# Expert weights in sheets of two pages with rows of 16 KB, GpSimd's work of the attention moved to VectorE, and a last norm summed in PSUM

## The chip, the cores and the metric
The kernel runs on one core of a Trainium2 chip. The core has five engines: TensorE (PE, matmuls; PEld is its weight load), VectorE (DVE), ScalarE (ACT), GpSimd (POOL) and SyncE (SP, which here issues nearly all DMA transfers). Sixteen DMA engines move data between HBM and SBUF. The metric is the device time of one execution in microseconds (us), the median of the runs. "us" positions are counted from the start of the profiled span.

## The reference
One encoder layer on 512 tokens of 1024 channels, all in float32. A conditioning vector gives shift, scale and gate rows for both halves (`sh, sc, g`). The first half is attention with two groups of heads (8 latent heads, 4 differential heads with a relative-position bias), an output projection and a layer norm. The second half is what the change touches most:

```
u   = x * (1 + sc_f) + sh_f
aff = softmax(u @ w_router)                      # 16 experts
g, idx = top_k(aff.T, 64)                        # each expert picks 64 of 512 tokens
xs  = u[idx]                                     # (16, 64, 1024)
h   = silu(xs @ w_gate) * (xs @ w_up)            # w_gate, w_up: (16, 1024, 2048)
y   = (h @ w_down) * g                           # w_down: (16, 2048, 1024)
ffn = zeros.at[idx].add(y)                       # back to the 512 tokens
out = layer_norm(ALPHA * x + g_f * ffn, ln2_g, ln2_b)
```

Each expert has three matrices of 8 MB, 403 MB in all, and each is read once.

## The kernel before, in words
SBUF is cut into 24 pages of 128 partitions x 8 KB (class `Pages`). Every larger tile takes a page or a half or quarter of one by `pages.get()` and gives it back by `pages.put()`; a page is the oldest free one.

**Up to the routing (0 to 340 us).** Stage 1 projects the input; then a loop over 32 steps `s` runs the scores, softmax and values of the 16 differential blocks (`s` 0 to 15) and the 16 latent blocks (`s` 16 to 31), with projections filled in between. Float32 operands of matmuls are split in a high and a low part (`split`: ACT rounds, another engine subtracts, L237). GpSimd subtracts for the queries (`q_proj`), the normalised latents (`lat_norm`), the value weights (`wk_load`) and the output weights (`wo_split`, which also multiplies by the gate row at L734). `W0, WD = 9, 3` say at which steps the first four blocks of the output weights are split (9, 12, 15, 18). This part has no order written by hand: the compiler's planner orders each engine's instructions by simulated times. From the second norm's sums on, sections marked `manual_schedule` keep the written order on each engine. The routing ends in a search of the 65th largest affinity (`DVE.max` and `match_replace`, L1192 to L1194) and the one-hot matrices that gather the chosen tokens.

**The experts (340 to 1278 us).** The 16 experts go in 8 pairs (`pr`); two experts of a pair use the two halves of TensorE's columns at once. For each pair, `up` runs eight blocks `k` of 128 channels for w_gate, then eight for w_up, and `down` eight blocks `b` of 256 FF rows for w_down. One block of one expert is 1 MB: one page, one DMA of 128 rows of 8 KB. Between blocks stand the scatter of the pair before (in the gate part), the gather of the next pair (in the down part) and the transposes of the hidden values (`hidden_t`). `prefetch` walks one list (`stream`, 392 loads) and issues the next load on SP whenever a page is free; `turn` gives back the pages of a used block and calls it. The list begins to move at `s` = 29 with `keep=3` pages left over, and after the routing with none. During pair 0 eight pages leave the stock for other tiles (tokens, gate rows, hidden values, their transposes, norm rows, two of accumulators; `take_xs` to `take_acc`); one comes back in pair 1. In the last pair w_down is read in two column halves for its second half (16 loads of 512 KB in rows of 2 KB).

**The last norm (`finish`).** After the last down matmul DVE gates the result, PE scatters it, and DVE, ACT and GpSimd share the sums, the inverse root and the scaling of the 512 x 1024 output; SP stores it in eight pieces.

Of the kernel before, what the change touches and what calls it, by code (L numbers as in the profile page):

```python
# [21 lines left out]
W0, WD = 9, 3  # L22
# [4 lines left out]
NPAGES = 24  # L27
NWARM = 384
# [25 lines left out]
class Pages:  # L54
    def __init__(self, pool, n):
        self.pool = pool
        self.t = [None] * n
        self.kind = [None] * n
        self.used = [0] * n
        self.stamp = [[0] * 4 for _ in range(n)]  # L60
        self.now = 0
        self.peak = 0

    def get(self, kb=8, kind=F32, old=False):
        need = kb // 2
        best = None
        for i, u in enumerate(self.used):
            if u and self.kind[i] != kind:
                continue
            for off in range(0, 4 - need + 1, need):  # L70
# [4 lines left out]
                key = (age, u == 0) if old else (u == 0, age)  # L75
# [5 lines left out]
        if not self.used[i]:  # L81
            self.now += 1
            self.kind[i] = kind
            self.t[i] = self.pool.tile([P, 2048], kind, name=f"pg{i}_{self.now}", tag=f"pg{i}", bufs=1)
# [3 lines left out]

    def put(self, h):
        i, m = h  # L90
        assert self.used[i] & m == m
        self.used[i] &= ~m
        self.now += 1
        for k in range(4):
            if m >> k & 1:
                self.stamp[i][k] = self.now

    def free(self):
        return sum(u == 0 for u in self.used)
# [3 lines left out]
def encoder_layer(ctx: ExitStack, tc: tile.TileContext, xT, x, wadaT, cvec, colp, rowp, rows, cst, pos, posr,  # L103
# [5 lines left out]
    pagep = ctx.enter_context(tc.tile_pool(name="pagep", bufs=1))  # L109
# [4 lines left out]
    pages = Pages(pagep, NPAGES)  # L114
# [492 lines left out]
    def lat_evac(j, bank):  # L607
# [5 lines left out]
        if j == 1:  # L613
            POOL.tensor_tensor(s, s, lat[0][3], op=OP.add)
# [28 lines left out]
    def wk_load():  # L643
# [3 lines left out]
        WK["vh"], WK["v"] = split(raw[:, 512:], 512, POOL)  # L647
# [54 lines left out]
    def q_proj(h, bank):  # L702
# [8 lines left out]
        QM[h] = split(f, 512, DVE if h < 0 else POOL)  # L711
# [28 lines left out]
    def x_load():  # L740
        for t2 in range(2):
            h, pg = pages.get()
# [20 lines left out]
    Gc, Bc = fixed.tile([P, 8], F32, name="Gc"), fixed.tile([P, 8], F32, name="Bc")  # L763
    wrg = rowb[:, :256].rearrange("p (k e) -> p k e", k=KB)
# [147 lines left out]

# [14 lines left out]

    NP = NEXP // 2
    stream = []
    for pr in range(NP):  # L930
        for w, nm in ((w_gate, "g"), (w_up, "u")):
            for k in range(KB):
                for e in range(2):
                    off = w.offset + ((2 * pr + e) * D + k * P) * FF
                    stream.append(((pr, nm, k, e), bass.AP(tensor=w.tensor, offset=off, ap=[[FF, P], [1, FF]])))
        for b in range(KB if pr < NP - 1 else KB // 2):
            for e in range(2):
                off = w_down.offset + ((2 * pr + e) * FF + b * 2 * P) * D
                stream.append(((pr, "d", b, e), bass.AP(tensor=w_down.tensor, offset=off, ap=[[2 * D, P], [1, 2 * D]])))

    for c in range(2):
        for b in range(KB // 2, KB):
            for e in range(2):
                off = w_down.offset + ((2 * (NP - 1) + e) * FF + b * 2 * P) * D + c * 512
                stream.append(((NP - 1, c, b, e), bass.AP(tensor=w_down.tensor, offset=off, ap=[[2 * D, P], [D, 2], [1, 512]])))
    stream.reverse()
    loaded = {}

    def prefetch(keep=0):
        while stream and pages.free() > keep:  # L950
            key, src = stream.pop()
            n = math.prod(src.shape[1:])
            h, pg = pages.get(n // 256)
            SP.dma_start(pg.rearrange("p (j n) -> p j n", j=2) if len(src.shape) == 3 else pg, src)
            loaded[key] = (h, pg)
# [101 lines left out]
    for s in range(NU):  # L1057
# [42 lines left out]
        if s in MODS or s >= 18:  # L1100
            mod_step()
        if s in EARLY:
            prefetch(EARLY[s])
# [26 lines left out]
    prefetch(KEEP)  # L1130
# [53 lines left out]
    prefetch()  # L1184
# [5 lines left out]

    for r in range(8):
# [36 lines left out]
    def gather(pr, banks, k0=0, k1=KB):  # L1228
        oh = OHh[0].rearrange("p (t s) -> p t s", t=4)
        xs = XS[pr % 2]  # L1230
        for k in range(k0, k1):
            src = banks[k % 2][:, (k // 2) * P:(k // 2 + 1) * P]
            for t in range(4):
                mm(src, Z[t][:, k * P:(k + 1) * P], oh[:, t, :], t == 0, t == 3)
            if k % 2:
                ACT.activation(xs[:, k, :], src, AF.Identity, scale=Gc[:, k:k + 1], bias=Bc[:, k:k + 1])
            else:
                DVE.tensor_scalar(xs[:, k, :], src, Gc[:, k:k + 1], Bc[:, k:k + 1], op0=OP.mult, op1=OP.add)  # L1238
# [36 lines left out]
    def take_rows():  # L1275
        EP["gbh"], gb = pages.get()
        EP["gb"] = gb
# [22 lines left out]
    def last_rows():  # L1300
        _, l2 = pages.get()
        SP.dma_start(l2[0:1, :], bass.AP(tensor=rows.tensor, offset=rows.offset + 2048, ap=[[2048, 1], [1, 2048]]))
        EP["l2"] = l2
# [12 lines left out]
    def up(pr, nm, banks, between, columns=None):  # L1316
# [269 lines left out]
```

## Time and profile before

| what | value |
|---|---|
| time, median of 3 runs | 1303.66 us (1299.6 to 1304.99) |
| time of the profiled execution | 1303.92 us |
| its span, first to last instruction | 1302.1 us |
| mean granted TensorE clock | 0.969 |
| busy: PE, DVE, ACT, POOL | 1185.2, 373.8, 225.0, 118.7 us |
| moved by DMA | 456.1 MB, mean 350 GB/s |

A row of the profile names an engine, a line of the kernel (L12 is line 12), what is written and read, and the number of instructions. "Busy" counts time in instructions; for PE it is not the same as work at full rate. The granted clock is 1.00 at 2.4 GHz and 0.50 at 1.2 GHz.

### The profile page before, as it was taken

Reading aid. Unit: us, or ns where it says so; the run is one execution under the profiler, and the core shown is the slowest. Engines: PE = TensorE matmul, PEld = TensorE weight load, DVE = VectorE, ACT = ScalarE, POOL = GpSimd, SP = SyncE. Lnnn points to the kernel's source line nnn. Section 1 sums busy time; section 2 is a strip of 40 time slices with the busy share of each in tenths; the row PEclk is TensorE's granted clock in tenths of the full one; section 3 lists DMA queues with packets and bytes.
Section 4 is the critical chain, followed back from the end, with each engine's and each line's share of the span. In section 5 each row is a group of like instructions: output and inputs, shape, how many; then the busy total and the mean of one; then the engine's idle time right before and its main releaser. Section 6 shows DMA issues by size and latency. Waiting matters only on the chain.

```text
span 1302.1 us, 13908 instructions
## 1 busy us (share of the span) xinstructions
PE 1185.2 (91%) x5581; PEld 550.5 (42%) x5581; DVE 373.8 (29%) x793; ACT 225.0 (17%) x464; POOL 118.7 (9%) x79
## 2 busy tenths in 40 slices
PE   8899888999899999998899799879978997998793
PEld 5677556777433433432342243224323432432231
DVE  6798897636301111020110012010101110110107
ACT  3465665542210000000000000000000000000000
POOL 2500532320000500000000000000000000000002
PEclk9899998999999999999999999999998999999987
DMA  9775531374999899999999999999999999999981
GB/s 345 291 231 194 176 138 65 130 283 154 385 385 420 335 422 421 421 421 421 421 422 421 421 422 421 421 421 421 422 421 421 420 421 422 421 422 421 422 304 65
DMA packets 76215, 456.10 MB, mean 350 GB/s; under 512 B 8140, under 2 KB 8524, under 8 KB 28018
## 3 DMA queue, kind: packets, MB, share of 16 engines
q1 hardware_dynamic: 75858, 455.08, 86.3%
q8 instruction: 44, 0.72, 0.2%
q14 instruction: 23, 0.19, 0.0%
q10 hardware_dynamic: 290, 0.10, 0.0%
HBM read 453.04 MB, written 3.95 MB: 351 GB/s over the span
## 4 chain that ended last, share of the span: by engine, by line
DMA 45%; PE 27%; DVE 2%; issue 0%; ACT 0%; SPq 0%; DVEq 0%
DMA pg<-in_w_up_dram 19%; DMA pg<-in_w_gate_dram 15%; PE bk L122 14%; PE bk L1322 11%; DMA pg<-in_w_down_dram 11%; PE bk L1353 1%; DVE pg L1427 0%; DVE pg L1418 0%; DVE small L1192 0%; DVE ohg L1194 0%; DVE lst L1412 0%; DVE lst L162 0%; PE bk L1243 0%; DVE mv L165 0%; PE bk L1271 0%
## 5 line engine op out<-in xcount | busy, mean ns | idle before, releaser
L122 PE MATMUL bk<-pg,pg 128*128 128x512 f32 (+4 forms) x2282 | 530.9, 490 | 13.6 <-POOL pg L423 4.4
L122 PEld LDWEIGHTS bk<-pg,pg 128*64 128x64 f32 (+2 forms) x2282 | 259.7, 163 | 237.5 <-issue 176.3
L1322 PE MATMUL bk<-pg,pg 128*64 128x512 f32 x1024 | 242.8, 609 | 35.1 <-DMA pg<-in_w_up_dram 33.6
L1322 PE MATMUL bk<-pg,xs 128*64 128x512 f32 x1024 | 241.0, 605 | 30.3 <-DMA pg<-in_w_up_dram 30.0
L1322 PEld LDWEIGHTS bk<-pg,pg 128*64 128x64 f32 x1024 | 73.6, 139 | 193.3 <-issue 128.5
L1322 PEld LDWEIGHTS bk<-pg,xs 128*64 128x64 f32 x1024 | 73.3, 138 | 183.0 <-issue 124.3
L1347 DVE TENSOR_TENSOR pg<-pg,bk 128x512 f32<-128x512 f32 x32 | 22.0, 688 | 405.0 <-PE bk L1322 405.0
L144 ACT ACTIVATE pg<-bk 128x512 f32<-128x512 f32 (+1 forms) x105 | 59.3, 583 | 434.2 <-PE bk L1353 353.7
L1226 POOL TENSOR_TENSOR ohg<-ohg,aff 128x512 f32<-128x512 f32 x8 | 8.4, 1049 | 789.5 <-DVE ohg L1225 789.5
L1249 DVE TENSOR_TENSOR pg<-pg,bk 128x512 f32<-128x512 f32 x60 | 41.3, 688 | 124.7 <-PE bk L122 124.4
L122 PEld LDWEIGHTS bk<-ohg,pg 128*128 128x128 f32 x512 | 61.3, 196 | 28.8 <-issue 28.8
L122 PE MATMUL bk<-ohg,pg 128*128 128x128 f32 x512 | 67.9, 286 | 0.5 <-DVE ohg L1225 0.5
L1343 ACT ACTIVATE pg<-bk 128x512 f32<-128x512 f32 x32 | 18.8, 598 | 241.3 <-PE bk L1322 241.3
L137 ACT ACTIVATE pg<-pg 128x512 fp32r<-128x512 f32 (+2 forms) x63 | 42.8, 708 | 26.0 <-DVE pg L710 7.0
L237 POOL TENSOR_TENSOR pg<-pg,pg 128x512 fp32r<-128x512 f32 (+1 forms) x20 | 34.8, 1745 | 91.6 <-ACT pg L137 91.5
L1008 DVE CUSTOM_DVE_ANT_0 pg<-pg,pg 128x1024 f32<-128x1024 f32 x32 | 39.7, 1276 | 2.3 <-DMA pg<-in_wadaT_dram 2.2
L1238 DVE TENSOR_SCALAR xs<-bk,Gc,Bc 128x128 f32<-128x128 f32 x16 | 6.6, 410 | 100.1 <-PE bk L122 100.1
L1238 DVE TENSOR_SCALAR pg<-bk,Gc,Bc 128x128 f32<-128x128 f32 x16 | 6.6, 410 | 97.7 <-PE bk L122 97.7
L122 PE MATMUL bk<-pg 64*128 64x512 f32 (+3 forms) x94 | 30.5, 485 | 3.2 <-DMA pg<-in_cvec_dram 2.2
L1386 DVE TENSOR_TENSOR pg<-bk,pg 128x512 f32<-128x512 f32 x16 | 11.1, 692 | 67.5 <-PE bk L122 67.5
L1353 PEld LDWEIGHTS bk<-csb,pg 128*128 128x128 f32 x128 | 17.8, 209 | 26.1 <-issue 22.8
L218 DVE CUSTOM_DVE_ANT_0 pg<-pg,pg 128x1024 f32<-128x1024 f32 x16 | 25.7, 1640 | 5.7 <-DMA pg<-in_wadaT_dram 5.7
(211 smaller groups left out, 629.4 us busy)
## 6 DMA issues: line engine op xcount, KB each, us to landing
pg<-in_w_gate_dram SPq DMA_DIRECT2D x128, 1024.0 KB, 19.8
pg<-in_w_up_dram SPq DMA_DIRECT2D x128, 1024.0 KB, 19.8
pg<-in_w_down_dram SPq DMA_DIRECT2D x120, 1024.0 KB, 19.8
pg<-in_wadaT_dram SPq DMA_DIRECT2D x16, 1024.0 KB, 7.3
pg<-in_wadaT_dram SPq DMA_DIRECT2D x16, 512.0 KB, 6.2
pg<-in_w_down_dram SPq DMA_DIRECT2D x16, 512.0 KB, 10.8
pg<-bias_d SPq DMA_DIRECT2D x16, 256.0 KB, 4.8
pg<-in_w_out_dram SPq DMA_DIRECT2D x8, 512.0 KB, 3.2
```

What stands on the lines that cost most here:

```text
L122: PE.matmul(o, l, r, start=start, stop=stop)
L137: return ACT.activation(dst, src, AF.Copy, scale=scale)
L144: ACT.activation(dst, src, AF.Copy)
L218: DVE.tensor_tensor_reduce(out=w2[:, j], in0=w2[:, j], in1=cs, scale=1.0, scalar=0.0, op0=OP.mult, op1=OP.add, accum_out=modr[:, n:n + 1])
L237: lo_eng.tensor_tensor(lo, src, ff(hi), op=OP.subtract)
L1008: DVE.tensor_tensor_reduce(out=w2[:, j], in0=w2[:, j], in1=cs, scale=1.0, scalar=0.0, op0=OP.mult, op1=OP.add, accum_out=modr[:, n:n + 1])
L1238: DVE.tensor_scalar(xs[:, k, :], src, Gc[:, k:k + 1], Bc[:, k:k + 1], op0=OP.mult, op1=OP.add)
L1249: DVE.tensor_add(acc[t][:, c], acc[t][:, c], bank)
L1322: PE.matmul(banks[c][r], xs[:, k, r], w[e][:, c * 512:(c + 1) * 512], start=k == 0, stop=k == 7)
L1343: ACT.activation(EP["HS"][:, c * 512:(c + 1) * 512], banks[c], AF.Silu)
L1347: DVE.tensor_tensor(s, s, U[c], op=OP.mult)
L1353: PE.transpose(G[c % 2][:, i * P:(i + 1) * P], sj[:, i // 2, i % 2, :], ident)
```

## The change
**Sheets.** From the top of the 24 pages, two neighbouring free pages are turned into a "sheet" of 128 partitions x 16 KB the first time one is wanted. One load of the stream is now 2 MB: partition p holds two neighbouring channels of w_gate or w_up (256 channels in a block), or four neighbouring FF rows of w_down (512 in a block), 16 KB in one run. The tokens are gathered with every second column (`k // 2 * 256 + k % 2 :: 2`) and the hidden values transposed with every fourth, so that the contraction fits; the gate scale and shift columns are regrouped for it (`GBp`). A sheet is used in two halves and given back after the second. The lowest ten pages (`LOW`) serve other tiles; pages 0 and 1 are kept for x, and from step 18 (`LATE`) tiles are put into the low pages first. In the first fill a 2 MB load may also go to two low pages as two DMAs of 8 KB rows; later loads go to sheets. The page of the first norm's rows is kept and reloaded with the last norm's rows (`l2`).

**GpSimd.** All its subtractions, products and the sum between stage 1 and the routing go to DVE; `W0, WD = 15, 1` splits the first output weights at steps 15 to 18.

**The end.** The last norm's rows are spread to all partitions in gate step 6 of the last pair (before: behind down block 1). In `finish` each token block's first half is multiplied by the norm's scale row early, and its bias and mean terms are summed by matmuls with diagonal matrices in PSUM; DVE does the second halves; GpSimd is not used.

The diff, cut:

```diff
-W0, WD = 9, 3
+W0, WD = 15, 1
+LOW = 10
+LATE = 18
 class Pages:
-    def get(self, kb=8, kind=F32, old=False):
+    def get(self, kb=8, kind=F32, old=False, first=2, top=None):
...
-                key = (age, u == 0) if old else (u == 0, age)
+                high = self.late and (0 if i < self.low else i - self.low + 1)
+                key = (age, u == 0) if old else (high, u == 0, age) if self.late else (u == 0, age)
...
+    def has_sheet(self):
+        n = len(self.used)
+        return any(not u for u, _, _ in self.sheets) or n > self.low and not self.used[n - 1] and not self.used[n - 2]
+    def sheet(self):
+        free = [x for x in self.sheets if not x[0]]
+        if free:
+            x = min(free, key=lambda x: x[1])
+        else:
+            for v in (self.used, self.stamp, self.t, self.kind):
+                del v[-2:]
+            self.pools.pop().release()
+            i = len(self.sheets)
+            x = [0, 0, self.open(f"sheet{i}", bass.Side.RIGHT if hasattr(bass.Side, "RIGHT") else "right")]
+            self.sheets.append(x)
...
-            POOL.tensor_tensor(s, s, lat[0][3], op=OP.add)
+            DVE.tensor_tensor(s, s, lat[0][3], op=OP.add)
-        LN_[j] = split(c, 512, POOL)
+        LN_[j] = split(c, 512, DVE)
-        WK["vh"], WK["v"] = split(raw[:, 512:], 512, POOL)
+        WK["vh"], WK["v"] = split(raw[:, 512:], 512, DVE)
-        QM[h] = split(f, 512, DVE if h < 0 else POOL)
+        QM[h] = split(f, 512, DVE)
-        POOL.tensor_tensor(raw, raw, GR["r"], op=OP.mult)
-        WOh[k], WO[k] = split(raw, 1024, POOL)
+        DVE.tensor_tensor(raw, raw, GR["r"], op=OP.mult)
+        WOh[k], WO[k] = split(raw, 1024, DVE)
...
+    def block(w, ex, rows, b, n):
+        return bass.AP(tensor=w.tensor, offset=w.offset + (ex * rows + b * n * P) * (4096 // n), ap=[[4096, P], [1, 4096]])
...
+    def prefetch(keep=0, low=0):
+        while stream and (not keep or pages.free() - 2 * (not begun) >= keep):
+            key, src = stream[-1]
+            if not begun and pages.has_sheet() and not (low == 2 and pages.free(LOW)):
+                h, pg = pages.sheet()
...
+            elif (begun or low) and pages.free(LOW):
+                h, pg = pages.get(top=LOW)
+                SP.dma_start(pg, bass.AP(tensor=src.tensor, offset=src.offset + 2048 * len(begun), ap=[[4096, P], [1, 2048]]))
...
-            prefetch(EARLY[s])
+            prefetch(EARLY[s], 1)
-    prefetch(KEEP)
+    prefetch(KEEP, 1)
-    prefetch()
+    prefetch(0, 2)
+    for h in range(2):
+        for j in range(2):
+            for i, v in enumerate((Gc, Bc)):
+                mm(BK[4][64 * h:64 * h + 64, 8 * i + j:8 * i + j + 7:2], ident[:, j:127 + j:2], v[:, h:h + 7:2], True, True)
...
-            (0, "u", 5): take_rows, (0, "d", 2): lambda: take_acc(0), (0, "d", 4): lambda: take_acc(1),
-            (1, "g", 0): lambda: pages.put(EP["gbh"]), (NP - 1, "g", 7): last_rows}
+            (0, "u", 5): take_rows, (0, "d", 1): lambda: take_acc(0), (0, "d", 3): lambda: take_acc(1),
+            (NP - 2, "d", KB - 1): last_rows}
...
+        n = KB if columns is None else KB - 1
+        for k in range(KB):
+            if k % 2 == 0:
+                h, w = zip(*(loaded.pop((pr, nm, k // 2, e)) for e in range(2)))
...
+            turn(pr, nm, k, h[0][k % 2] + h[1][k % 2])
...
+    def finish_first(t):
         scatter(NP - 1, t, 0, TB[t % 2])
+        a = acc[t][:, :512]
+        DVE.bn_stats(lst[:, 24 * t:24 * t + 6], a)
+        DVE.tensor_tensor(a, a, EP["l2"][:, :512], op=OP.mult)
     def finish():
...
+        bias(0)
+        gated(1, YB)
+        bias(1)
+        for t in range(4):
+            mm(LB[t], OHT[(NP - 1) % 2][:, t * P:(t + 1) * P], EP["YS"][:, 512:], False, True)
+            DVE.bn_stats(lst[:, 24 * t + 6:24 * t + 12], LB[t])
+            DVE.bn_aggr(mv2[:, 2 * t:2 * t + 2], lst[:, 24 * t:24 * t + 12].rearrange("p (c s) -> p c s", s=6))
...
+        for t in range(4):
+            ACT.activation(diag[:, t], ident, AF.Copy, scale=nb[:, t:t + 1])
+            mm(banks[t], diag[:, t], l2[:, :512], False, t == 3)
+            if t < 3:
+                ACT.activation(diag[:, 4 + t], ident, AF.Copy, scale=rs[:, t:t + 1])
+                mm(banks[t], diag[:, 4 + t], acc[t][:, :512], False, True)
+        for t in range(4):
+            centre(t)
+            scaled(t)
...
+            elif k == 6 and pr == NP - 1:
+                spread(EP["l2"], U[2:], (1.0, 1.0))
...
-                if b == 1:
-                    spread(EP["l2"], TB, (1.0, 1.0))
```

## Rows read from the trace of the kernel before
**Rows 1.** Windows: PE, PEld, DVE, ACT, POOL busy (count), granted clock, DMA share, GB/s.
```profile
500.00:1100.00 600.00, 546.89 (x2468) 202.44 (x2464) 65.46 (x105) 30.06 (x55) 5.25 (x5) 0.99 1.01 421
```
**Rows 2.** Chain that ended last: start us, length us, what.
```profile
488.90 15.62 DMA pg<-in_w_up_dram
...
1207.35 17.35 DMA pg<-in_w_up_dram
```
**Rows 3.** Window in the down part of pair 0.
```profile
430.00:440.00 10.00, 10.00 (x62) 5.53 (x60) 0.82 (x2) 0.92 (x2) 4.42 (x3) 1.00 0.76 288
```
**Rows 4.** Window of the loads with rows of 2 KB.
```profile
1247.00:1259.00 12.00, 12.00 (x38) 3.56 (x38) 0.69 (x1) 0.00 (x0) 0.00 (x0) 0.82 1.05 387
```
**Rows 5.** Timeline of SP's issues: start us, length us, count.
```profile
271.77 51.40 SPq L954 DMA_DIRECT2D pg<-in_w_gate_dram  x13
...
456.61 32.68 SPq L954 DMA_DIRECT2D pg<-in_w_up_dram  x16
```
**Rows 6.** Timeline of PE, pairs 0 and 1; a step is 16 matmuls.
```profile
366.05 7.09 PE L1322 MATMUL bk<-pg,xs 128*64 128x512 f32 x32
...
444.91 7.09 PE L122 MATMUL bk<-pg,pg 128*64 128x512 f32 x32
...
458.01 3.65 PE L1322 MATMUL bk<-pg,pg 128*64 128x512 f32 x16
```
**Rows 7.** Timeline of PE, last pair; in brackets idle before and its releaser.
```profile
1199.87 8.78 PE L1322 MATMUL bk<-pg,pg 128*64 128x512 f32 x32 [2.40 <-DMA pg<-in_w_up_dram]
...
1242.44 5.29 PE L122 MATMUL bk<-pg,csb 1*128 1x512 f32 x8
1247.66 5.50 PE L122 MATMUL bk<-pg,pg 128*64 128x512 f32 x16
1253.09 1.98 PE L122 MATMUL bk<-pg,csb 128*128 128x512 f32 x4
```
**Rows 8.** Timeline of DVE, last norm.
```profile
1278.12 0.69 DVE L1386 TENSOR_TENSOR pg<-bk,pg 128x512 f32<-128x512 f32 x1 [0.46 <-PE bk L122]
...
1287.39 1.23 DVE L165 TENSOR_SCALAR mv<-mv 128x2 int32<-128x2 int32 x1
...
1298.34 0.68 DVE L1435 TENSOR_TENSOR pg<-pg,pg 128x512 f32<-128x512 f32 x1
```
**Rows 9.** Windows of the tail.
```profile
1240.00:1250.00 10.00, 10.00 (x26) 2.91 (x24) 1.38 (x2) 1.19 (x2) 0.00 (x0) 0.73 1.04 390
...
1290.00:1302.00 12.00, 0.00 (x0) 0.00 (x0) 8.92 (x15) 0.78 (x1) 4.29 (x3) 0.50 0.41 154
```
**Rows 10.** Groups by line: names, shapes, count | busy us, mean ns | idle before.
```profile
L237 POOL TENSOR_TENSOR pg<-pg,pg 128x512 fp32r<-128x512 f32 (+1 forms) x20 | 34.8, 1745 | 91.6 <-ACT pg L137 91.5
...
L734 POOL TENSOR_TENSOR pg<-pg,pg 128x1024 f32<-128x1024 f32 x8 | 21.0, 2635 | 11.6 <-DMA pg<-in_w_out_dram 10.3 <-ACT pg L144 1.3
...
L237 DVE TENSOR_TENSOR pg<-pg,pg 128x1024 fp32r<-128x1024 f32 x7 | 9.4, 1361 | 1.5 <-ACT pg L137 1.5
```
**Rows 11.** Timelines of DVE and PE, 120 to 210 us.
```profile
122.61 1.35 DVE L162 TENSOR_TENSOR st<-st 128x4 f32<-128x4 f32 x2
...
146.72 2.30 DVE L168 SCALAR_TENSOR_TENSOR small<-small 128x8 f32<-128x8 f32 x1
...
149.07 1.11 PE L631 MATMUL bk<-csb,small 128*128 128x128 f32 x4 [3.99 <-DVE small L168]
...
208.79 2.20 DVE L571 SCALAR_TENSOR_TENSOR pg<-pg,st,rowb 128x128 f32<-128x128 f32 x4
```
**Rows 12.** Windows, 120 to 320 us.
```profile
120.00:180.00 60.00, 52.10 (x298) 37.77 (x298) 52.83 (x130) 38.94 (x95) 29.11 (x15) 0.97 0.40 136
180.00:220.00 40.00, 32.11 (x175) 23.15 (x175) 33.80 (x79) 20.57 (x48) 2.65 (x2) 0.87 0.35 126
220.00:320.00 100.00, 100.00 (x692) 78.21 (x688) 52.72 (x121) 46.52 (x107) 25.20 (x12) 1.00 0.47 177
```
**Rows 13.** Timeline of PE: four transposes with step two.
```profile
1228.83 0.75 PE L1353 MATMUL bk<-csb,pg 128*128 128x128 f32 x4
```

More of the change, by code (lines that the diff above doesn't have):

```diff
@@ L54, with __init__ @@
 class Pages:
-    def __init__(self, pool, n):
-        self.pool = pool
+    def __init__(self, tc, ctx, n, low):
+        self.tc, self.ctx, self.low = tc, ctx, low
+        self.pools = [self.open(f"pages{i}", bass.Side.LEFT if hasattr(bass.Side, "LEFT") else "left") for i in range(n // 2)]
+        self.sheets = []
         self.t = [None] * n
@@ L62, in __init__, with open @@
         self.peak = 0
-    def get(self, kb=8, kind=F32, old=False):
+        self.late = False
+    def open(self, name, side):
+        pool = self.tc.tile_pool(name=name, bufs=1, side=side).__enter__()
+        self.ctx.callback(lambda: pool._released or pool.release())
+        return pool
+    def get(self, kb=8, kind=F32, old=False, first=2, top=None):
         need = kb // 2
         best = None
-        for i, u in enumerate(self.used):
-            if u and self.kind[i] != kind:
+        for i, u in enumerate(self.used[:top]):
+            if i < first or u and self.kind[i] != kind:
                 continue
@@ L87, in get @@
         return (i, m), self.t[i][:, off * 512:(off + need) * 512]
+    def has_sheet(self):
[12 more added lines that the diff above has]
+            self.sheets.append(x)
+        i = next(j for j, y in enumerate(self.sheets) if y is x)
+        self.now += 1
+        x[0] = 1
+        return ("sheet", i), x[2].tile([P, 4096], F32, name=f"sh{i}_{self.now}", tag=f"sh{i}", bufs=1)
     def put(self, h):
         i, m = h
+        self.now += 1
+        if i == "sheet":
+            assert self.sheets[m][0]
+            self.sheets[m][:2] = [0, self.now]
+            return
         assert self.used[i] & m == m
         self.used[i] &= ~m
-        self.now += 1
         for k in range(4):
@@ L96, in put, with free @@
                 self.stamp[i][k] = self.now
-    def free(self):
-        return sum(u == 0 for u in self.used)
+    def free(self, top=None):
+        return sum(u == 0 for u in self.used[:top])
 @with_exitstack
@@ L741, in x_load @@
         for t2 in range(2):
-            h, pg = pages.get()
+            h, pg = pages.get(first=0, top=2)
             Zh.append(h)
@@ L941, in encoder_layer @@
     for c in range(2):
[L942 to L945, printed above, removed]
+        for b in range(2, 4):
+            stream.append(((NP - 1, c, b), [bass.AP(tensor=w_down.tensor, offset=w_down.offset + ((2 * (NP - 1) + e) * FF + b * 512) * D + c * 512,
+                                                    ap=[[4 * D, P], [D, 4], [1, 512]]) for e in range(2)]))
@@ L946, in encoder_layer @@
     stream.reverse()
     loaded = {}
[L949 to L955, printed above, removed]
+    begun = []
+    def prefetch(keep=0, low=0):
[3 more added lines that the diff above has]
+                h, pg = pages.sheet()
+                if isinstance(src, list):
+                    for e in range(2):
+                        SP.dma_start(pg[:, e * 2048:(e + 1) * 2048].rearrange("p (j n) -> p j n", j=4), src[e])
+                else:
+                    SP.dma_start(pg, src)
+                loaded[key] = ([[], [h]], [pg[:, :2048], pg[:, 2048:]])
+                stream.pop()
+            elif (begun or low) and pages.free(LOW):
+                h, pg = pages.get(top=LOW)
+                SP.dma_start(pg, bass.AP(tensor=src.tensor, offset=src.offset + 2048 * len(begun), ap=[[4096, P], [1, 2048]]))
+                begun.append((h, pg))
+                if len(begun) == 2:
+                    loaded[key] = ([[x] for x, _ in begun], [x for _, x in begun])
+                    begun.clear()
+                    stream.pop()
+            else:
+                break
```

163 lines of the change are left out of this document (62 added, 101 removed).

## The prediction, written before the change was run

> **What bounds the kernel now.** I read the page's slices first, then the windows, the chain of waits, SP's issues, and last the timelines of PE and DVE at both ends. From about 450 us to 1260 us the DMA engines are full: over 500 to 1100 us their share is 1.01 at 421 GB/s, while PE is busy 547 of 600 us [rows 1]. The chain there is one weight transfer after another; PE takes it over once the last w_up page has landed, at 1207.35 + 17.35 = 1224.7 us [rows 2]. That instant is the hinge: before it DMA sets the time; behind it PE needs 53.3 us to the end of the last down matmul (1278.0, just ahead of the DVE row at 1278.12 that reads its bank), and the last norm another 24.1 us to the span's end at 1302.1 [rows 2, 7, 8]. Ahead of it lies the stretch to 340 us in which PE and DVE do attention and routing, and one from 340 to 450 us in which PE is the slower one and the transfers stand still for want of pages: 288 GB/s at 430 to 440 [rows 3]. So a change pays by (a) an earlier routing, (b) a better rate while DMA is full, (c) less standing still, (d) a shorter tail. The sum is made on the profiled execution's 1303.9 us, 1.8 above its span and 0.3 above the median of the three runs; 0.5% or 6.5 us is about what a measurement of this kernel can tell from no change.
>
> **Row length (b).** A page now moves as 128 rows of 8 KB, a sheet as 128 rows of 16 KB. Each of 16 engines carries eight rows of a 1 MB page: 8192 B at 421/16 GB/s are 311.3 ns a row. The last stretch of 2 KB rows ran at 387 GB/s, 84.7 ns a row [rows 1, 4]. 6 KB more cost 226.6 ns, so 2 KB cost 75.5 and 9.2 ns is fixed for each row. With half as many rows a page's worth saves 8 x 9.2 / 2 = 37 ns (613 ns a row of 16 KB, 427 GB/s). From page 80, landed at 488.90 + 15.62 = 504.5 us (SP's sixteenth w_up issue of pair 1 is the one at 488.9), to page 368 at 1224.7 us [rows 2, 5] are 288 pages: **-10.6 us**. Below lies no gain (a 16 KB row may be cut into two transfers of 8 KB), above twice as much if the 9.2 is an underestimate; I take the straight line through both rows.
>
> **Sheets instead of pages (c).** Before, after 8 pages have been taken for other tiles, 16 remain for weights, freed one by one. After, 14 pages make seven sheets; a sheet holds two blocks of rows and is freed when the second is used; the low ten pages are not filled again behind the first fill. So sheet n can be issued when n - 7 are used up. PE's rows give the uses: the last down block of pair 0 ends at 444.91 + 7.09 = 452.0 us, the sixth and fourth some 9 and 20 us before it (each step of 3.6 us has a gather of 2 with it),  pair 1's first gate pair at 458.01 + 3.65 = 461.7, the next about 11 us later [rows 6]. Kindest walk: the first fill is in sheets and DMA is stopped only by this limit. Sheets 26 and 27 go at 432, then pairs at 443, 452, 461.7 and 472.6; a pair takes 9.8 us, so sheet 35 lands at 482.4 and from there the queue never empties; sheet 40 (page 80) lands at 482.4 + 24.5 + 2 = 508.9, 4.4 us late. Harshest: the first four weight blocks lie in low pages, whose release frees nothing; all eleven have landed by about 347 and DMA waits until gate step 5 ends at 366.05 + 3.6 = 369.6 us; from there it is full, and 29 sheets later it is 369.6 + 142.3 + 2 = 513.9, 9.4 us late. I take **+7**. Later the pair of sheets in use lasts PE 7.1 to 11 us and five sheets hold 24 us of transfers, so this costs nothing again; if PE stood still over 13 us, it would.
>
> **Gate rows spread earlier (d).** The spread of the last norm's rows costs 5.29 us on PE in the down part of the last pair, and it leaves the clock at 1.2 GHz: the next 16 matmuls take 5.50 against 3.65 us, and the window has 0.73 granted [rows 6, 7, 9]. Gone from there: 7.1 us. It now stands in gate step 6 of the last pair, under DMA: a pair's 48 pages take it 117.7 us, and PE is busy 547/600 of the 119.5 they took before, 109 us [rows 1], so 8.7 are free; if that cover is gone the 7 come back. DMA is late next: behind the last w_up page 8 MB in 16 KB rows (19.7 us) and 8 MB in 2 KB rows (21.7 at 387 GB/s) end at +41.4; the last sheet then feeds 2 x 1.8 us of matmuls and a scatter of 1.0: +46, against PE's own 53.3 - 7.1 = 46.2. So **-6.5**.
>
> **Last norm (d).** Before, DVE's last instruction ends 1299.02 - 1278.0 = 21.0 us behind the last down matmul [rows 8]; of these about 5 are DVE instructions of 1.2 to 1.8 us that take 0.16 to 0.75 elsewhere, all while POOL works, as the row of 1.23 us. After: scatter add, statistics and product of block 3 and the gate in DVE's order end at 3.8; four accumulating matmuls and statistics to 8.5; eleven small steps of 0.2 to 10.7; then DVE's eight operations to 16.4, while PE runs seven matmuls of 0.86 from 11.2 to 17.5; the last fused product ends near 18.3. **-2.5** (bounds: -4 if gating is drawn ahead as before, +3 if PE's seven run at 1.2 GHz).
>
> **POOL's work to DVE (a).** 20 splits, 8 products of 1024 and one sum: on POOL 34.8 + 21.0 us [rows 10]; on DVE, at 0.69 for 512 and 1.36 for 1024 columns, 13 x 0.69 + 16 x 1.36 = 31 us. What DVE gets back is the blocking: a step on 128x8 took 2.30 us at 146.72, where such steps take 0.2, and PE waited 3.99 us for it. Twelve lengthened instructions, the first in the row at 122.61 and the last in that at 208.79, come to 16.7 us over their usual time [rows 11]. DVE was busy 52.8 of 60 and 33.8 of 40 us between 120 and 220, PE 52.1 and 32.1 [rows 12]; what DVE takes over there (nine operations of 512, eight of 1024) comes to 6.2 + 10.9 = 17.1. Load stays equal, but the four W_out blocks move late (steps 15 to 18), so the waits before 180 go and some come at 180 to 220. From 220 to 320 PE is busy 100 of 100 us and DVE 53; 14 more on DVE fit. Against it: allocation from step 18 keeps to ten low pages, and pages 0 and 1 wait for x. I take **-3**, ends -16 (all PE idling of 120 to 220) and +5.
>
> **Small edits.** Eight small matmuls and a copy for the regrouped gate columns: PE has only filling matmuls to do while DVE searches; 0, at most 1. The norm's rows are loaded in an existing page a pair earlier: one issue of 0.3 us on SP before two queued sheets; 0. The acc steps one block earlier: under PE's down part; 0, at most 4.7. Transposes now take every fourth column; every second cost 0.75 for four [rows 13]; 16 lie behind the hinge: 0, at most +3 if doubled. The Trainium skill, "SBUF — State Buffer", Specifications, wants two hits for each 16-byte line, which a step of four floats misses: by it those +3 would be paid, and no row here shows it.
>
> Sum: 1303.9 - 10.6 + 7 - 6.5 - 2.5 - 3 = 1288.3; **1288.5 us** with 0.2 for the transposes.
>
> **Rivals.** *Rate unchanged* (16 KB rows cut in two): the gain of 10.6 goes, and the walks lose 1 more: 1300. For it: nothing in the trace shows a row above 8 KB. *Late filling*: upper pages still hold tenants when the first fill is due, sheets need the top two free, and the stream starts with the routing. Before, 13 page loads were issued between 271.77 and 323.2 us [rows 5]. From 326 us without a pause sheet 40 lands at 326 + 40 x 4.91 + 2 = 524.3, 19.8 late in place of 7, and an earlier routing gives nothing: 1304. *Tight pages, the other side*: from step 18 the short tiles of attention turn in eight low pages, so each of 14 steps between 220 and 320, where PE now never waits, waits for evictions of the step before. Two of 512 columns (2 x 0.69 us as on DVE [rows 8]) a step are 19 us, four 39; with the other terms (-12.4) that ends at 1310.5 to 1330. It decides from 1.3 us a step on. Against it: program order already releases before it takes. *Routing much earlier*: all PE idling of 120 to 220 goes (15.8 us): 1276. *Cold array in the norm*: PE idles twice for 2 us there and its clock was at 0.50 in the last 12 us [rows 9]; seven matmuls at 1.2 GHz end 6 us later: 1295. The Trainium skill, "TensorE: Matmul & The Clock Gate", HAM oscillation, says that waits for data throw the array back to half rate in every tile; a wait of 2.40 us was followed by 32 matmuls in 8.78 us [rows 7], where 32 took 7.09 [rows 6], so it agrees. Sheets make such waits the rule (9.8 - 7.1 = 2.7 us each), but 8.8 stays below 9.8, so it takes nothing off DMA's pace.
>
> **Chances.** Forecast 0.46 (1282 to 1297), much earlier 0.12, cold array 0.08: faster 0.66. Rate unchanged 0.13 and late filling 0.11: same 0.24. Tight pages 0.10: slower. The range reaches from 1275 to 1305, over all but the last, less half of the earliest case's own spread.
>
> **What would show it.** Steady GB/s 427 and 24,000 rows of 16 KB (right) or 421 (wrong). Gate step 5 begun before 366 us. Page 80 by 505 to 511 us. No 1-row matmuls and no 0.73 behind the last w_up landing, 46 us from there to the last down matmul; 18 us from it to DVE's end. Most wrong would be PE waits appearing between 220 and 320, or DMA share under 1.0 behind 500 us.

## The result, and the profile after

The changed kernel took 1285.64 us (median of four runs, 1283.91 to 1287.08) against 1304.02 us, a ratio of 0.987 with a 95% interval of 0.984 to 0.989. The forecast was 1288.5 us, faster. The profiled execution took 1287.08 us, its span 1285.3. Its windows (columns as in [rows 1]):

```profile
120.00:180.00 60.00, 53.94 (x274) 37.87 (x273) 54.78 (x158) 35.48 (x85) 0.00 (x0) 0.92 0.40 132
180.00:220.00 40.00, 38.62 (x239) 29.75 (x238) 35.11 (x83) 28.46 (x68) 0.00 (x0) 0.99 0.21 67
220.00:320.00 100.00, 97.34 (x707) 75.39 (x705) 64.13 (x156) 44.85 (x106) 0.00 (x0) 1.00 0.52 196
...
273.00:333.00 60.00, 55.73 (x393) 40.55 (x392) 38.50 (x133) 24.72 (x61) 0.78 (x1) 0.94 0.83 332
333.00:513.00 180.00, 177.41 (x820) 69.05 (x819) 18.84 (x31) 13.69 (x24) 20.01 (x10) 0.98 0.93 384
...
500.00:1100.00 600.00, 550.52 (x2445) 208.22 (x2443) 65.70 (x105) 30.08 (x55) 5.23 (x5) 0.98 1.01 427
```

The steady stream moves 427 GB/s at the same DMA share of 1.01 [rows 1 had 421]. Ahead of it GpSimd is idle, and PE is busy 38.62 of 40 us between 180 and 220, where it had 32.11 [rows 12]. From 333 to 513 DMA isn't full: a share of 0.93, the stand-still that the forecast charged to the sheets. It ends at about 393 us, as two shorter windows show; below them the kernel before:

```profile
373.00:393.00 20.00, 20.00 (x96) 6.79 (x94) 0.00 (x0) 0.00 (x0) 0.00 (x0) 1.00 0.65 246
393.00:413.00 20.00, 20.00 (x86) 7.25 (x84) 5.71 (x9) 2.39 (x4) 2.54 (x2) 1.00 1.01 430
```

```profile
333.00:513.00 180.00, 178.89 (x838) 70.84 (x836) 23.38 (x49) 14.45 (x26) 20.80 (x10) 0.98 0.96 392
```

The chain of waits (start, length) has the landing of the last w_up sheet of pair 1, the counterpart of page 80 [rows 2]:

```profile
487.29 16.76 DMA sh<-in_w_up_dram
```

PE's timeline has the first gather (the matmuls that collect the chosen tokens), the first matmul on the last w_up sheet, four transposes of hidden values, the wait for the second pair of down sheets, the scatter behind the last down matmul, and the norm:

```profile
332.28 3.06 PE L159 MATMUL bk<-ohg,pg 128*128 128x128 f32 x24 [0.50 <-DVE ohg L1290]
...
1213.25 5.36 PE L1385 MATMUL bk<-sh,pg 128*64 128x512 f32 x22 [2.71 <-DMA sh<-in_w_up_dram]
1218.60 0.75 PE L1410 MATMUL bk<-csb,pg 128*128 128x128 f32 x4
...
1233.35 3.65 PE L159 MATMUL bk<-sh,pg 128*64 128x512 f32 x14 [1.52 <-DMA sh<-in_w_down_dram]
...
1261.84 1.13 PE L159 MATMUL bk<-pg,pg 128*128 128x512 f32 x2
...
1265.80 3.70 PE L159 MATMUL bk<-pg,pg 128*128 128x512 f32 x8 [1.12 <-DVE pg L1446]
...
1273.15 7.97 PE L159 MATMUL bk<-pg,pg 128*128 128x512 f32 x14 [1.94 <-ACT pg L1494]
```

The first gather of the kernel before:

```profile
339.84 2.92 PE L122 MATMUL bk<-ohg,pg 128*128 128x128 f32 x24 [0.50 <-DVE ohg L1225]
```

These instants cut both spans into pieces. In the table, "pair 1" is the landing of its last w_up transfer, "last w_up" that of the last pair, and "last down" the end of the last down matmul, each read at the transfer's landing or at the PE or DVE row that follows it. In brackets is what the piece ahead of the instant lost or gained against the kernel before.

| | first gather | pair 1 | last w_up | last down | end of span |
|---|---|---|---|---|---|
| before | 339.84 | 504.5 | 1224.7 | 1278.0 | 1302.1 |
| changed | 332.28 (-7.6) | 504.05 (+7.1) | 1213.25 (-11.0) | 1261.84 (-4.7) | 1285.3 (-0.6) |

Together -16.8 us. Gate step 5 of pair 0 begins at 358.9 us (forecast: before 366), and 49,588 - 24,946 = 24,642 packets of the page's count have 8 KB or more (forecast: 24,000 rows of 16 KB).

### The profile page after: what moved, and what is told of

It is laid out like the page before. It is cut to its first block, busy times and chain, and to the rows that moved or that the text cites. A ratio compares the mean times of both kernels' runs of the same rounds, so it can differ in the third digit from the quotient of the medians.

```text
span 1285.3 us, 13557 instructions
## 1 busy us (share of the span) xinstructions
PE 1198.6 (93%) x5619; PEld 564.4 (44%) x5619; DVE 375.7 (29%) x813; ACT 226.9 (18%) x472; POOL 54.5 (4%) x45
## 2 busy tenths in 40 slices
DMA packets 49588, 456.06 MB, mean 355 GB/s; under 512 B 5068, under 2 KB 5452, under 8 KB 24946
## 4 chain that ended last, share of the span: by engine, by line
PE 53%; DMA 21%; DVE 1%; issue 0%; ACT 0%; DVEq 0%
PE bk L159 27%; PE bk L1385 23%; DMA sh<-in_w_up_dram 16%; DMA sh<-in_w_down_dram 5%; PE bk L1410 1%; PE bk L1260 1%; PE bk L1308 0%; DVE lst L1485 0%; PE bk L1336 0%; DVE mv L1486 0%; DVE pg L1506 0%; DVE lst L1457 0%; ACT aff L876 0%; DVE ohg L1290 0%; DVE pg L1404 0%
## 5 line engine op out<-in xcount | busy, mean ns | idle before, releaser
L159 PE MATMUL bk<-pg,pg 128*128 128x512 f32 (+3 forms) x1274 | 308.0, 401 | 14.2 <-POOL pg L460 4.4
L1385 PE MATMUL bk<-sh,pg 128*64 128x512 f32 x1024 | 240.1, 614 | 25.0 <-DMA sh<-in_w_up_dram 25.0
L1385 PE MATMUL bk<-sh,xs 128*64 128x512 f32 x960 | 231.1, 611 | 27.1 <-DMA sh<-in_w_up_dram 27.1
L159 PE MATMUL bk<-sh,pg 128*64 128x512 f32 x1024 | 239.9, 601 | 3.6 <-DMA sh<-in_w_down_dram 3.6
L159 PEld LDWEIGHTS bk<-pg,pg 128*128 128x128 f32 (+2 forms) x1274 | 193.5, 183 | 113.1 <-issue 57.1
L1385 PEld LDWEIGHTS bk<-sh,pg 128*64 128x64 f32 x1024 | 76.4, 140 | 177.8 <-issue 139.3
L1385 PEld LDWEIGHTS bk<-sh,xs 128*64 128x64 f32 x960 | 71.5, 140 | 167.4 <-issue 128.0
L1404 DVE TENSOR_TENSOR pg<-pg,bk 128x512 f32<-128x512 f32 x32 | 21.9, 687 | 379.6 <-PE bk L1385 379.6
L159 PEld LDWEIGHTS bk<-sh,pg 128*64 128x64 f32 x1024 | 72.4, 137 | 136.9 <-issue 122.4
L274 DVE TENSOR_TENSOR pg<-pg,pg 128x512 fp32r<-128x512 f32 (+1 forms) x40 | 36.9, 932 | 17.7 <-ACT pg L174 17.7
L1065 DVE CUSTOM_DVE_ANT_0 pg<-pg,pg 128x1024 f32<-128x1024 f32 x32 | 38.0, 1220 | 4.2 <-DMA pg<-in_wadaT_dram 4.2
L1303 DVE TENSOR_SCALAR pg<-bk,GBp 128x128 f32<-128x128 f32 x16 | 6.6, 411 | 106.5 <-PE bk L159 106.5
L159 PE MATMUL bk<-pg 64*128 64x512 f32 (+2 forms) x92 | 29.8, 482 | 3.2 <-DMA pg<-in_cvec_dram 2.2
```

The costliest lines, as they stand in the source:

```text
L159: PE.matmul(o, l, r, start=start, stop=stop)
L274: lo_eng.tensor_tensor(lo, src, ff(hi), op=OP.subtract)
L1065: DVE.tensor_tensor_reduce(out=w2[:, j], in0=w2[:, j], in1=cs, scale=1.0, scalar=0.0, op0=OP.mult, op1=OP.add, accum_out=modr[:, n:n + 1])
L1303: DVE.tensor_scalar(xs[:, k, :], src, GBp[:, 0, k:k + 1], GBp[:, 1, k:k + 1], op0=OP.mult, op1=OP.add)
L1385: PE.matmul(banks[c][r], xs[:, k, r], w[e][:, c * 512:(c + 1) * 512], start=k == 0, stop=k == 7)
L1404: DVE.tensor_tensor(s, s, U[c], op=OP.mult)
```

## The experiments

Each run stood beside runs of the kernel before; ratios are to those. The differences in us are between spans of profiled executions unless medians are named. One execution differs from the next: in the six kernels that do the same as the changed one up to the last pair (it, the one with the spread put back, and the four of the tail) the first gather lies between 330.73 and 334.78 us, so a difference of up to 4 us in one instant can be scatter.

**Row length or transfer size?** Two kernels bring back rows of 8 KB (their code is shortened here). The first fills a sheet by two transfers:

```
-SP.dma_start(pg, src)
+for i in range(2):
+    SP.dma_start(pg[:, i*2048:(i+1)*2048], AP(src + 2048*i, [[4096, P], [1, 2048]]))
```

> The changed kernel, with each 2 MB sheet filled by two transfers of 1 MB with rows of 8 KB. Theory (the length of a row sets the rate): the stretch from 500 to 1100 us moves 421 GB/s instead of 427, packets of 8,192 bytes, about +10 us: 1295 to 1297 us. Rival (sheets, or anything else of the change, raised the rate): 427 GB/s stays, 1285 to 1288 us.

The second keeps one transfer of 2 MB and cuts its rows; the sheets then hold other rows than they should, so only its time is of use:

```
+rows8 = AP(src, [[2048, P], [2048 * P, 2], [1, 2048]])
+SP.dma_start(pg.rearrange("p (j n) -> p j n", j=2), rows8)
```

> The changed kernel, with each 2 MB sheet still filled by one transfer, but its rows cut in two of 8 KB that lie 1 MB apart (the weights reach other rows of the sheet, so the experts compute something else in the same time). Theory (row length): 421 GB/s and 1295 to 1297 us, as with two transfers. Rival (number of transfers: half as many issues, semaphores and completions raised the rate): 427 GB/s and 1285 to 1288 us.

Two transfers: 1297.13 us, ratio 0.996 (0.9945 to 0.997). One transfer: 1298.47 us, 0.996 (0.995 to 0.998). Their windows, first and second kernel:

```profile
500.00:1100.00 600.00, 551.51 (x2422) 211.09 (x2420) 65.66 (x105) 30.05 (x55) 5.24 (x5) 0.97 1.01 420
```

```profile
500.00:1100.00 600.00, 548.99 (x2412) 206.79 (x2410) 65.70 (x105) 30.07 (x55) 5.24 (x5) 0.97 1.01 420
```

Both medians lie just above what the theory gave (1295 to 1297). Both kernels fall to 420 GB/s at a full DMA share, and the piece from pair 1 to the last w_up grows from 709.2 to 720.4 and 722.1 us, the 720.2 of before. The length of a row sets the rate; half as many transfers (2 MB instead of 1 MB each) bring nothing. The term is shown with its size.

**The routing.** Six lines of attention went from GpSimd to DVE, and the splits of the output projection from steps 9, 12, 15, 18 to 15, 16, 17, 18. First both were undone in the changed kernel (the steps to 10, 13, 16, 19, since at 9 there is no page for them in the new layout), and both done alone in the kernel before:

```
-W0, WD = 15, 1                         # changed kernel; the reverse in the kernel before, from 9, 3
+W0, WD = 10, 3
-LN_[j] = split(c, 512, DVE)            # and five more lines
+LN_[j] = split(c, 512, POOL)
```

> The changed kernel, with the six lines back on GpSimd and the output projection's splits at steps 10, 13, 16, 19 (before: 9, 12, 15, 18; the first of these finds no page in the new layout). Theory (the earlier routing is worth what it is early, since the sheets' lead is lost behind it whatever its time): first gather 7 to 8 us later, page 80's counterpart (sheet 40) at 511 to 512 us, 1292 to 1294 us. Rival (the stream's stand-still at 340 to 380 us takes the delay in): first gather 7 to 8 us later, sheet 40 at 504 to 507 us, 1285 to 1289 us.

> The kernel before, with only the six lines moved from GpSimd to DVE and the output projection's splits at steps 15 to 18. Theory (the earlier routing is worth its time by itself): first gather at 332 to 334 us instead of 339.8, last w_up's counterpart of pair 1 at 497 us instead of 504.5, 1296 to 1298 us. Rival (before, the stream had no stand-still there, so its bytes and not the routing set page 80's landing): first gather as early, page 80 at 502 to 504.5 us, 1300 to 1304 us.

Then each half was undone by itself:

> The changed kernel, with the six lines back on GpSimd and the output projection's splits left at steps 15 to 18. With both halves undone (e3) the first gather came 12.2 us later and the time was 19 us more. Theory (the engine of the six lines is the main part: GpSimd takes longer for each and slows DVE's beside it): first gather 6 to 10 us later, at 338 to 342 us, 1294 to 1300 us. Rival (the steps of the splits are the main part): first gather under 4 us later, at 332 to 336 us, 1285 to 1291 us.

> The changed kernel, with the splits back at steps 10, 13, 16, 19, on DVE. Theory (engine of the six lines): first gather under 4 us later, at 332 to 336 us, 1285 to 1291 us. Rival (steps): first gather 6 to 10 us later, 1294 to 1300 us.

| | median, ratio (interval) | first gather | pair 1 | last w_up | end |
|---|---|---|---|---|---|
| both undone | 1304.68, 1.001 (1.000 to 1.002) | 344.46 | 521.8 | 1232.5 | 1302.6 |
| kernel before, both done | 1293.50, 0.992 (0.991 to 0.994) | 333.77 | 496.7 | 1216.6 | 1294.2 |
| GpSimd's lines undone | 1305.47, 1.002 (1.001 to 1.003) | 349.05 | 520.8 | 1231.5 | 1301.4 |
| steps undone | 1306.10, 1.002 (1.001 to 1.004) | 345.82 | 522.2 | 1233.0 | 1304.8 |

First gather and pair 1 of the four kernels, in the table's order:

```profile
344.46 3.07 PE L159 MATMUL bk<-ohg,pg 128*128 128x128 f32 x24 [0.50 <-DVE ohg L1290]
...
521.82 5.36 PE L1385 MATMUL bk<-sh,pg 128*64 128x512 f32 x22 [1.03 <-DMA sh<-in_w_up_dram]
```

```profile
333.77 2.92 PE L122 MATMUL bk<-ohg,pg 128*128 128x128 f32 x24 [0.50 <-DVE ohg L1225]
...
481.21 15.47 DMA pg<-in_w_up_dram
```

```profile
349.05 3.06 PE L159 MATMUL bk<-ohg,pg 128*128 128x128 f32 x24 [0.50 <-DVE ohg L1290]
...
520.83 7.06 PE L1385 MATMUL bk<-sh,pg 128*64 128x512 f32 x22 [2.21 <-DMA sh<-in_w_up_dram]
```

```profile
345.82 3.06 PE L159 MATMUL bk<-ohg,pg 128*128 128x128 f32 x24 [0.50 <-DVE ohg L1290]
...
522.27 5.36 PE L1385 MATMUL bk<-sh,pg 128*64 128x512 f32 x22 [2.71 <-DMA sh<-in_w_up_dram]
```

All four medians lie outside both ranges that were expected of them. In the kernel before, the two edits bring the first gather 6.1 us forward, the landing of pair 1 7.8 and the end 7.9 (10.3 by the medians). In the changed kernel, undoing either or both puts the first gather 12 to 17 us back, and the end 16 to 19.5 back (19 to 20.5 by the medians). So neither half is the main part, as both theories of the last pair had it: in the changed kernel each is worth nothing without the other, and the rest of the change is worth nothing in sum without this routing (1304.68 against 1303.84 for the kernel before in those runs). Its pieces against the kernel before are +4.6 to the first gather, +12.7 from there to pair 1, -9.5 to the last w_up and -7.3 behind it: the gains behind pair 1 stay, and the stretches ahead of it take them back.

The halves cost in different places. With GpSimd's lines back alone, the piece from the first gather to pair 1 is 171.8 us, as in the changed kernel; its whole loss lies ahead of the first gather. With the old steps that piece grows too, to 177.4 us (both undone) and 176.4 (steps alone).

Two mechanisms show. With GpSimd's lines back, its work on the output weights falls together at steps 15 to 18. GpSimd, DVE and PE of that kernel, from the timelines:

```profile
189.37 2.39 POOL L771 TENSOR_TENSOR pg<-pg,pg 128x1024 f32<-128x1024 f32 x1 [3.08 <-ACT pg L566]
191.72 6.38 POOL L274 TENSOR_TENSOR pg<-pg,pg 128x1024 fp32r<-128x1024 f32 x3
```

```profile
189.81 1.96 DVE L202 TENSOR_SCALAR st<-st 128x4 int32<-128x4 int32 x1
...
192.30 2.29 DVE L199 TENSOR_TENSOR st<-st 128x4 f32<-128x4 f32 x1
...
195.74 2.37 DVE L575 SCALAR_TENSOR_TENSOR st<-sts,small,st 128x1 f32<-128x1 f32 x1
...
199.86 0.16 DVE L205 SCALAR_TENSOR_TENSOR st<-st 128x4 f32<-128x4 f32 x1
```

```profile
199.81 2.07 PE L159 MATMUL bk<-pg,pg 128*128 128x512 f32 x4 [7.49 <-DVE pg L735]
```

While GpSimd works, these three steps of DVE on one or four columns last 1.96 to 2.37 us; right behind, such a step takes 0.16. PE waits 7.49 us for what DVE has queued behind them. An earlier wait and the windows of this kernel show what comes on top:

```profile
155.00 1.12 PE L581 MATMUL bk<-csb,pg 128*128 128x128 f32 x4 [4.18 <-DVE pg L576]
```

```profile
140.00:160.00 20.00, 15.82 (x69) 12.29 (x68) 13.15 (x30) 9.64 (x22) 11.09 (x6) 0.76 0.39 117
160.00:180.00 20.00, 18.51 (x62) 10.15 (x62) 16.91 (x47) 10.87 (x28) 3.62 (x3) 0.67 0.19 62
180.00:200.00 20.00, 12.29 (x63) 8.81 (x62) 17.93 (x27) 11.83 (x27) 12.39 (x6) 0.84 0.09 31
```

The wait of 4.18 us ends at 155.0; the granted clock is 0.67 from 160 to 180, which is two thirds of that stretch at 1.2 GHz. The changed kernel had 0.91, 0.94 and 0.97 in these three windows. How much of the 16.8 us each of the two takes was not measured. The Trainium skill, "GPSIMD Engine Reference", Specifications, names SBUF interfaces that GpSimd shares with VectorE, with contention for DVE instructions in a 2-port mode or with two SBUF inputs; the two steps with two inputs agree with that (2.29 and 2.37 us), and whether the one with one input (1.96 us) ran in a 2-port mode the rows don't show.

With the old steps there is a delay in SP's queue as well. Its waits, of the kernel with both undone (line, what it waited for: us in total, times, longest):

```profile
SPq L1005 <- PE bk L159: 51.7, 5, 18.9
SPq L766 <- PE bk L159: 34.1, 1, 34.1
```

SP stands 34.1 us at the last load of W_out (issued at 273.93) until PE frees its page, and the first weight load, queued behind it, waits again and goes out at 292.43 instead of 273.05 (274.92 and 294.10 with the steps alone undone). The windows:

```profile
273.00:333.00 60.00, 57.24 (x432) 43.17 (x431) 31.14 (x107) 27.04 (x67) 7.03 (x3) 0.99 0.27 92
333.00:513.00 180.00, 176.38 (x814) 70.71 (x816) 26.21 (x60) 19.14 (x33) 20.78 (x10) 0.96 1.01 425
```

92 GB/s ahead of the routing against 332, and a full share from 333 us on: this is the rival "late filling" as it was written, with the first load into a sheet at 330.56 us against its 326, and 521.8 us for pair 1 against its 524.3. What exactly delays the first gather by 13.5 us when DVE does the splits at the old steps isn't taken apart; PE's waits there are many small ones.

**The spread of the last rows**, back behind down block 1:

```
-elif k == 6 and pr == NP - 1:            # gate step
-    spread(EP["l2"], U[2:], (1.0, 1.0))
+if b == 1:                               # down part of the last pair
+    spread(EP["l2"], TB, (1.0, 1.0))
```

> The changed kernel, with the spreading of the last norm's rows back behind down block 1 of the last pair (two banks instead of two banks of the other half at gate step 6). Theory (the spread stood on the path behind the last w_up landing: 5.3 us of one-row matmuls and a stretch at half clock behind them): last w_up landing to last down matmul 53 to 54 us instead of 48.6, +4 to +7 us, 1290 to 1293 us. Rival (PE waits for the down sheets anyway, 1.5 us at the second pair): the spread fits partly before that landing, +0 to +2.5 us, 1285.5 to 1288 us.

1290.16 us, 0.990 (0.989 to 0.992): 4.5 us over the changed kernel's median, as the theory had it. The profiled execution is the slowest of the six (1296.73): from the last w_up landing (1216.95) to the last down matmul (1271.53) it takes 54.6 us instead of 48.6. PE's timeline:

```profile
1216.95 7.06 PE L1385 MATMUL bk<-sh,pg 128*64 128x512 f32 x22 [2.71 <-DMA sh<-in_w_up_dram]
...
1235.91 4.85 PE L159 MATMUL bk<-pg,csb 1*128 1x512 f32 x8
1240.70 5.98 PE L159 MATMUL bk<-sh,pg 128*64 128x512 f32 x16
```

The spread brings 4.8 us of one-row matmuls, and a block of 5.98 us at a granted clock of 0.61 instead of 3.65; against it the 2.8 us are gone that PE loses to the late down sheets in the changed kernel (the wait of 1.52 us and the slower blocks around it). 4.8 + 2.3 - 2.8 = 4.3, as the medians say. The other 1.7 of the 6.0 lie ahead of the spread: behind the same wait of 2.71 us the 22 matmuls on the last w_up sheet took 7.06 us here (granted clock 0.76) and 5.36 in the changed kernel (1.00).

**One sheet less**: the number of pages that never become sheets is 12 instead of 10.

> The changed kernel, with 12 pages kept out of the sheets instead of 10: six sheets instead of seven for the steady stream. Theory (what can be loaded ahead of the first gather sets where the stream stands when it becomes continuous): 2 MB less ahead, 4.9 us at 427 GB/s; sheet 40 lands at 508 to 510 us, 1289.5 to 1292 us, the rate from 500 us on still 427 GB/s. Rival (the stream makes it up): within 1.5 us of the changed kernel. A second rival (six sheets don't hide PE's pauses between the phases): DMA share under 1.0 after 500 us and over 1295 us.

1295.35 us, 0.994 (0.992 to 0.995), 3 us above the theory's range; the rate after 500 stays 427 GB/s at a share of 1.01, so the second rival isn't it either.

```profile
333.77 3.06 PE L159 MATMUL bk<-ohg,pg 128*128 128x128 f32 x24 [0.50 <-DVE ohg L1290]
...
512.07 6.79 PE L1385 MATMUL bk<-sh,pg 128*64 128x512 f32 x22 [2.72 <-DMA sh<-in_w_up_dram]
```

From the first gather to pair 1 it is 178.3 us instead of 171.8: +6.5, of which 4.9 were expected. The DMA share from 333 to 513 is 0.88 instead of 0.93. What can be held ahead of the stream sets where it becomes continuous, and it isn't made up later. Why it is 1.6 us more than the bytes of one sheet was not taken apart.

**The tail.** Four kernels change the last norm: gating before block 3's sums; two more bias writes in PE's wait; gating first with the last half row block on DVE; and that with three bias writes.

```
+if b == 7:                               # e9: ahead of finish_first(3)
+    gated(1, YB)
+for t in (2, 3):                         # e10: ahead of bias(2), bias(3)
+    mm(banks[t], ident, l2[:, D:D + 512], True, True)
```

> The changed kernel, with the gating of the last 512 channels ahead of the scatter's sums of block 3 on DVE. Theory (the gating stands behind three DVE instructions of 0.7 us that nothing behind it needs first): the last scatter's matmuls begin 1.9 to 2.1 us earlier, 1283.5 to 1284 us. Rival (the later norm waits for block 3's sums and statistics all the same): within 0.5 us of the changed kernel.

> The changed kernel, with two more writes of the bias into the banks of rows 2 and 3 (0.94 us each, the same values) in the 1.9 us in which PE waits for the steps of the square root. Theory (PE's wait brings the half clock on the 14 matmuls behind it, 7.97 us instead of 6.0 to 6.2): clock 1.0 there, 1283.6 to 1284.4 us. Rival (the half clock comes from the waits further ahead, or comes anyhow): within 0.5 us of the changed kernel.

> The changed kernel, with the gating first and, for the last 128 rows, the first half of the norm in two DVE instructions instead of a bias and a diagonal matmul in PSUM. Expected of the sum of terms: -1.9 for the gating, and DVE's end 1.2 us earlier, since it waits 2.70 us for that matmul and then takes 0.75, against two instructions of 0.75 without a wait: 1282 to 1283 us. Rival (the first half of rows 2 on ACT and its store become the end): -1.9 us alone, 1283.5 to 1284 us.

> As the run before, with three more writes of a bias in PE's wait. If the half clock goes: 12 matmuls in 5.3 us instead of 7, 1281.5 to 1282.5 us; otherwise the same as without.

The medians are 1284.44, 1285.39, 1284.64 and 1285.44 us, ratios 0.986 to 0.987 with intervals of 0.005: none can be told from the changed kernel, and all four lie above what their theories gave. From the last down matmul to the end of the span it is 23.5 us in the changed kernel's profiled execution and 20.3, 21.7, 22.0 and 20.3 in these. PE's 14 (or 12) matmuls of the norm, in the order of the four kernels:

```profile
1271.93 6.28 PE L159 MATMUL bk<-pg,pg 128*128 128x512 f32 x14 [1.93 <-ACT pg L1495]
```

```profile
1273.17 6.28 PE L159 MATMUL bk<-pg,pg 128*128 128x512 f32 x14 [0.22 <-ACT pg L1496]
```

```profile
1270.50 7.11 PE L159 MATMUL bk<-pg,pg 128*128 128x512 f32 x12 [2.79 <-ACT pg L1495]
```

```profile
1272.63 5.42 PE L159 MATMUL bk<-pg,pg 128*128 128x512 f32 x12 [0.22 <-ACT pg L1497]
```

Much of this is the clock, and the clock changes without any edit to the norm. The other kernels above have the changed kernel's norm as it is. With two loads to a sheet:

```profile
1277.95 3.70 PE L159 MATMUL bk<-pg,pg 128*128 128x512 f32 x8 [1.12 <-DVE pg L1447]
...
1285.30 6.28 PE L159 MATMUL bk<-pg,pg 128*128 128x512 f32 x14 [1.93 <-ACT pg L1495]
```

These are the changed kernel's waits (1.12 and 1.94 us), and yet the 14 matmuls take 6.28 us instead of 7.97, at a granted clock of 1.00 instead of 0.79. So it is in four of the eight executions with this norm (two loads, short rows, both edits of the routing undone, GpSimd's lines undone: 6.28 us, and 21.7 to 21.9 from the last down matmul to the end); in the other four (changed kernel, steps undone, spread back, one sheet less) it is 7.97 us, and 23.4 to 23.9. That filling PE's wait keeps the clock up is therefore not shown: its 6.28 and its 21.7 us are those of an unchanged norm at full clock.

Against 21.7 at full clock, the gating put first is worth 1.4 us: it begins 0.3 us behind the last down matmul instead of 3.2, the wait of 1.12 us ahead of the scatter is gone, and the root's steps come 1.4 us sooner. Half a row block moved to DVE gains nothing (20.3 us with and without, both at full clock; the third kernel's 22.0 has a granted clock of 0.76 and 7.11 us for 12 matmuls instead of 5.42): at full clock DVE waits only 1.00 us for PSUM and takes 0.75, and two instructions of 0.75 come to about as much. A gain of 1.4 us is less than the medians of four or five runs can tell.

## Why the prediction came out

**Row length, -10.6: -11.0**, right in mechanism and size. The straight line through rows of 2 and 8 KB foretold 427 GB/s; 427 was measured, and 420 with rows of 8 KB whatever the transfer's size.

**Sheets' lead, +7: +7.1**, between its two walks. The kernel with one sheet less shows that this capacity is what the term hangs on. The path was neither walk's: the harshest had DMA full from 369.6 us on, the kindest held it back between 432 and 482, and in the trace it stood still in part until about 393 (0.65 from 373 to 393) and hardly after. So the capacity was right, and that the size fell in the middle is in part luck.

**Spread moved, -6.5: -4.7**, mechanism right. Undoing it by itself cost 4.3 to 4.5 us. The bound that comes next is DMA's, as written, but it bit at the first two pairs of down sheets (2.8 us, with the wait of 1.52 at 1233.35) and not at the last one; 48.6 us instead of 46.

**Last norm, -2.5: -0.6.** The mechanism stood, and at full clock the size too: 21.7 to 21.9 us against 24.1 before is -2.2 to -2.4. The rival of a cold array came true in part, in half of the executions with this norm: 7.97 us for PE's matmuls against 6.28, 1.7 us and not 6. The changed kernel's profiled execution is one of them; there DVE's end came 20.1 us behind the last down matmul instead of the 18.3 forecast.

**GpSimd to DVE, -3: -7.6** (6.1 by itself in the kernel before). This is the step that was mis-sized, and its reasoning was too simple. It weighed DVE's load and the lengthened steps, and took the rest of the kernel as given. The runs show that the gains of the other parts stand on this edit: in the changed kernel its absence costs 16 to 19.5 us, in the kernel before 7.9. The lead of +7 was worked out for early routing and a first fill that begins before it; with the old steps the same piece takes 177.4 us instead of 171.8. So the sum came out within 3 us because two terms held and the errors of the other three (-4.6, +1.8, +1.9) went against each other; that they did was luck.

**Small edits, 0.2.** The four transposes with every fourth column take 0.75 us at 1218.60, as those with every second did [rows 13]: nothing was paid for the longer step, and the 3 us didn't come.

**The rivals.** *Rate unchanged* fell to the window of 427. *Late filling* did not come, but it stands one edit away (the old steps), and close to its price: 1304.68 and 1306.10 us against 1304. *Tight pages*: PE waited 2.7 of 100 us between 220 and 320, far below what it needed. *Routing much earlier* had the sign right; half of it came. *Cold array*: its remark that the waits of the sheets bring the half clock held for some of them only (last section).

## What to carry to other kernels

Where DMA is full, the length of a row is worth a straight-line estimate from two row lengths in the trace; the number of transfers (1 MB or 2 MB each) changed nothing here. A buffer scheme that frees memory in larger pieces must be judged together with what runs ahead of its first use: the same change gave 17 us with one order of the work before its sheets and nothing with another. Undo parts one by one before calling one of them the cause; here both halves of an edit were needed. And look for the same stretch in every trace that has it unchanged before crediting an edit with it: the half clock in the norm came and went without one.

## What the hardware showed beyond what was expected

GpSimd's work lengthened DVE instructions on one or four columns per partition to about 2 us (0.16 otherwise), not only those with large operands. The TensorE clock did different things behind the same waits. Behind waits of 1.12 and 1.93 or 1.94 us in the norm, the granted clock of the next 14 matmuls was 0.79 in four executions and 1.00 in four others. In the steady stream of the changed kernel PE waits up to 2.7 us before each pair of w_up sheets; two such waits of one pair of experts, and the matmuls behind them:

```profile
828.72 8.78 PE L1385 MATMUL bk<-sh,xs 128*64 128x512 f32 x32 [2.17 <-DMA sh<-in_w_up_dram]
...
848.34 7.09 PE L1385 MATMUL bk<-sh,xs 128*64 128x512 f32 x32 [2.73 <-DMA sh<-in_w_up_dram]
```

The granted clock is 0.81 behind the shorter wait and 1.00 behind the longer one, and 0.98 over 500 to 1100 us. So the length of the last wait alone doesn't tell which level follows; what does stays open. The stream held 427 GB/s for 600 us; whether rows above 16 KB bring more stays open. The Trainium skill, "DMA: Bandwidth & Descriptors", Specifications, gives 435 GB/s as the ceiling of the fabric and about 358 as a core's limit at HBM; the rows come to 98% of the first and don't keep to the second.
